# 32 adaLN half tiles moved out of the attention heads, and the sparse heads' division put on ScalarE

## The chip, the cores and the metric

One core of a Trainium2 chip runs the whole program. The metric is the device time of one execution in microseconds (us), less being better; the time before is the median of three runs. Engines are named as in the profile: PE (TensorE matmul; PEld is its weight load), DVE (VectorE), ACT (ScalarE), POOL (GpSimd), SP (SyncE, which here issues most weight loads; SPq is its queue).

## The reference

One layer of a conditioned decoder trunk, 512 positions of width 2048, all in float32. Cut to what matters here:

```
c_act = silu(c)                                   # c: one row of 2048
mod = c_act @ w_ada + b_ada                       # 6 vectors of 2048
sh1, sc1, gt1, sh2, sc2, gt2 = split(mod, 6)
h = rmsnorm(x, g_mix) * (1 + sc1) + sh1
proj = h @ w_in                                   # q, k, v, indexer, gates
y_a = stick_breaking(q_a, k_a, v_a) @ w_a         # 8 heads
y_b = sparse(q_b, k_b, v_b, indexer) @ w_b        # 8 heads, softmax over the chosen keys
x = x + (1 + gt1) * ((sigmoid(g_a) * y_a + sigmoid(g_b) * y_b) @ w_o)
h = rmsnorm(x, g_ffn) * (1 + sc2) + sh2
x = x + (1 + gt2) * conv_ffn(h, w_up, conv_w, conv_b, w_down)
out = rmsnorm(x, g_final)
```

The change touches how `mod` is summed up (its part for sh1 and sc1 is done ahead of everything, and is not touched) and the last step of the sparse heads' softmax.

## The kernel before, in words

**Weights.** Every weight tile is 128x1024 floats (512 KB). SP loads it into a buffer `raw`, ACT rounds it to `wh` (`parts`, L133), DVE takes the rest `wl = raw - wh` (L135), and PE makes three matmuls for each pair of operands (`mm3`: L143 high by high, L144 high by low of the activations, L145 low by high). Activations are split in the same way (`split`, ACT L162 and DVE L164).

**Units.** The big projections run as `unit`s (L210 on). A unit takes four tiles a11, a21, a22, a12 and makes seven products of half the width in place of eight. It forms sums of its weight tiles on DVE: s = a21+a22 (L233), s - a11 (L237), a11 - a21 (L271), a12 - s (L275), and splits each, and it adds the products up on DVE: L241, L273, L274, L277, L279. The products are called by the activation form they use, in this order: B11, T1, T2, B21, T3, B22, T4. One product of the w_o stage is 24 matmuls.

**Buffers.** `raw` has 8 buffers, handed out in a ring. Two hold c, spread over the partitions, for as long as half tiles are to be done, so six go round. A load can be issued only when the last reader of the tile that held its buffer before is done, and SP issues in order.

**Half tiles.** `ada_half` (L287) does a piece of c_act @ w_ada: SP loads a 128x1024 piece of w_ada (L289) into a `raw` buffer and one DVE instruction multiplies it by c and adds it up (L290). 96 of these are left for the time beside the stages (`ada_left`); `some_ada(n)` does the next n of them. Nothing waits for a half tile but the next user of its buffer, until `mod` is needed. In the program's order they are placed by `behind(last)`, which sets the priority of what is issued in it right behind the instruction `last`; a scheduler then orders each engine's instructions before the run, and each engine runs its own in that order, waiting where it must.

**Stages**, in order, with the half tiles of each before the change:

- x units: 32 units of w_x (the input projection). `between(0)`, right behind the sum s, takes a step of side work (rotary tables, indexer; at the end, 6 half tiles through another buffer), `between(1)`, right behind the copy of the B21 product, a step and one half tile. 38 in all.
- stick-breaking heads: two for each of 8 heads, behind `stick_2` (L858), 16 in all.
- sparse heads: `sparse_1` (logits, maxima, Exp with the sums on ACT, L884), `sparse_2` (DVE: reciprocal of the sums L888, then the four blocks of the weights times it, L890), `sparse_3` (PE transposes, L899). Two half tiles ahead of `sparse_2` and two behind its last multiplication. 32 in all. Beside the heads PE does the product with w_a.
- merge: 16 column tiles j of the product with w_b; DVE multiplies by the gate (L964) and adds (L965). One half tile behind L965 for odd j below 12, 6 in all. Behind each odd j the forms for the w_o units are made (`form_t` L175 and L176, `form_u` L181 to L183, and splits).
- w_o: 8 units; `between` also turns a finished tile (four PE transposes). One half tile in `between(1)` while there are any, 4 in all, in units 0 to 3. L996 is the residual.
- then the norm, and the feed-forward stages, which the change does not touch.

The lines that the change and the prediction speak of: `ada_half` L287 to L290, `unit` L210 to L280, `between` of the x units L632 to L636, L858, `sparse_2` L887 to L891, L938 to L944, L964 to L970, `between` of w_o L989 to L993.

Of the kernel before, what the change touches and what calls it, by code (L numbers as in the profile page):

```python
# [14 lines left out]
AF = mybir.ActivationFunctionType  # L15
ALU = mybir.AluOpType
# [60 lines left out]
def block_kernel(ctx: ExitStack, tc: tile.TileContext, A: dict, out: bass.AP):  # L77
    nc = tc.nc
# [27 lines left out]
    act = nc.scalar.activation  # L106
    tt = nc.vector.tensor_tensor
    ts = nc.vector.tensor_scalar
# [183 lines left out]
    @contextmanager  # L292
    def behind(*pins):

        with ExitStack() as stack:
            for p in pins:
                stack.enter_context(tc.issue_after(p.ins))
            yield
# [158 lines left out]
    for c in range(2):  # L457
        w = prep(A["w_qi7"][c])
        for k in range(8):
            i = 8 * c + k  # L460
# [154 lines left out]
    def some_ada(n=1, tag=("raw", 8)):  # L615
        for _ in range(n):
            if ada_left:
                ada_half(cb, *ada_left.pop(0), tag)
# [11 lines left out]
    for u in range(32):  # L630

        def between(i, *pins):  # L632
            with behind(*pins):
                next(work)
                if i:
                    some_ada()  # L636

        pair = unit(A["w_x"][u], f, between)
        for i, o in enumerate(pair):
            if u >= 16:  # L640
                sig = act(o, o, AF.Sigmoid)
            save(xd[2 * u + i], o)
# [197 lines left out]
    for hd in range(NH):  # L840
        state = stick_1(hd)
        if hd + 1 < NH:
            pairs.append([fetch(xd[2 * hd + 2]), fetch(xd[2 * hd + 3])])
        if before:
            stick_4(*before, va)
            if hd % 4 == 0:
                va = [fetch(vd[hd + b]) for b in range(NQB)]
        run(fill, 1 if hd < 4 else 2)
        if hd == NH - 1:
            cosT, sinT = (fetch(rope_d[0][:, i * S : (i + 1) * S]) for i in range(2))  # L850
            fetch_pair(0)
            for i in range(4):
                ya[i] = fetch(yad[i])
        later, last = stick_2(*state)
        run(fill)
        with behind(last):
            run(index, 3)
            some_ada(2)  # L858
        before = hd, stick_3(*state, later)
        run(fill)  # L860
    run(index, 100)
# [23 lines left out]
        return p, s, last  # L885

    def sparse_2(p, s):  # L887
        nc.vector.reciprocal(s, s)  # L888
        for b in (2, 0, 1, 3):
            last = ts(p[b], p[b], s[:, b : b + 1], None, ALU.mult)  # L890
        return last  # L891

    def sparse_3(p):
# [37 lines left out]
    for hd in range(NH):  # L931
        p, s, last = sparse_1(*pairs[hd])
        if before:
            sparse_4(*before, y)
        if hd + 1 < NH:
            pairs.append(turned(hd + 1))
        run(fill)
        with behind(last):  # L938
            some_ada(2)
        last = sparse_2(p, s)  # L940
        run(fill)
        before = hd, sparse_3(p), vb[hd // 4]
        with behind(last):
            some_ada(2)  # L944
        run(fill, 2)
    sparse_4(*before, y)
    run(fill)
# [7 lines left out]
    for j in range(KT):  # L955
        t = t2k("w", 2)
        save(t, td[j])
        g = fetch(xd[33 + 2 * j])
        merged.append(g)
        ps = acc()  # L960
        w = prep(A["w_b"][j])
        for k in range(NH):
            mm3(ps, cols(w, k), y[k], k == 0, k == NH - 1)
        tt(g, ps, g, ALU.mult)  # L964
        last = tt(g, g, t, ALU.add)  # L965
        if j % 2:
            if j < 12:
                with behind(last):
                    some_ada()
            f += forms(merged.__getitem__, j // 2, j // 2 + 1)  # L970


# [16 lines left out]
    def between(i, *pins):  # L989
        turn()  # L990
        with behind(*pins):
            if i:
                some_ada()  # L993

    def residual(c, j, x, at=slice(0, S)):
        stt(c[:, at], c[:, at], mod[:, 32 + j : 33 + j], x[:, at], ALU.mult, ALU.add)  # L996
# [577 lines left out]
```

## Time and profile before

| what | value |
|---|---|
| median of 3 runs | 2814.03 us (2813.0 to 2816.05) |
| the profiled execution's own time | 2819.28 us |
| its span, first to last instruction | 2817.4 us |
| mean granted clock of TensorE | 0.997 |
| PE, DVE, ACT, POOL busy | 98%, 86%, 52%, 11% of the span |

The busy times are averages over some fifteen stages. A stage is read in a table of windows: length, busy time of each engine, and the granted clock, of one stretch. In the timeline of an engine each row is one instruction (or a run of like ones, "x3"): its start, its duration, engine, line, operation, the tiles that it writes and reads, and in brackets how long the engine had been idle and what released it. Instructions on one engine overlap a little, so the pitch from one start to the next is somewhat less than the duration. For SP a row is the issue of a transfer; when the transfer landed is in the view of a tile. The profiled execution took 5.25 us more than the median.

### The profile page before, as it was taken

What the parts mean: (1) busy time and instruction counts of PE and PEld (TensorE: products, weight loads), DVE (VectorE), ACT (ScalarE), POOL (GpSimd) and SP (SyncE); (2) the same over time, 40 slices, a digit from 0 to 9 for tenths busy, and PEclk for the clock granted to TensorE, in tenths of its full rate; (3) what the DMA queues carried; (4) which work ended last, traced back from release to release, by engine and by line L of the source; (5) the groups of instructions that cost most, each with busy time, mean ns of one, the idle gap of its engine ahead of it and who ended that gap; (6) DMA issues with size and microseconds to landing.
All of it is one profiled execution on the core that took longest, in us unless ns stands there. A gap on an engine that the chain in (4) does not pass through costs nothing.

```text
span 2817.4 us, 47873 instructions
## 1 busy us (share of the span) xinstructions
PE 2763.3 (98%) x18780; PEld 2535.6 (90%) x18780; DVE 2427.0 (86%) x3464; ACT 1467.8 (52%) x2066; POOL 314.8 (11%) x519
## 2 busy tenths in 40 slices
PE   9999999999999999999999999999999999999997
PEld 6769999999998777889999999999999999887875
DVE  8979889888897899788878989898989897888886
ACT  5554444455556665434456555555555455546452
POOL 0100000000102011111220100000000000002022
PEclk9999999999999999999999999999999999999998
DMA  9964456655567457866763566666666436568786
GB/s 357 336 228 143 157 182 202 215 160 178 169 208 235 129 196 265 269 222 192 211 223 118 176 168 171 168 172 171 170 169 168 134 111 204 166 180 234 203 250 195
DMA packets 164045, 549.56 MB, mean 195 GB/s; under 512 B 21398, under 2 KB 21782, under 8 KB 163820
## 3 DMA queue, kind: packets, MB, share of 16 engines
q1 hardware_dynamic: 116076, 404.82, 45.0%
q0 software_dynamic: 47152, 141.30, 18.0%
q8 instruction: 147, 2.41, 0.4%
q14 instruction: 78, 0.64, 0.1%
q10 hardware_dynamic: 592, 0.39, 0.0%
HBM read 453.19 MB, written 89.83 MB: 193 GB/s over the span
## 4 chain that ended last, share of the span: by engine, by line
PE 73%; DVE 6%; DMA 4%; issue 3%; ACT 1%; POOL 0%; DVEq 0%; POOLq 0%; ACTq 0%; SPq 0%
PE att L145 12%; PE att L143 12%; PE att L144 12%; PE acc L145 10%; PE acc L143 10%; PE acc L144 10%; DVE wl L135 1%; DMA raw<-in_w_x 1%; PE acc L709 1%; PE acc L803 1%; PE outs L909 1%; DMA F<-sumd 1%; DMA F<-x1d 1%; PE acc L878 1%; DMA raw<-in_w_down 1%
## 5 line engine op out<-in xcount | busy, mean ns | idle before, releaser
L133 ACT ACTIVATE wh<-raw 128x1024 fp32r<-128x1024 f32 (+2 forms) x795 | 835.5, 1052 | 1039.2 <-PE acc L144 195.6
L135 DVE TENSOR_TENSOR wl<-raw,wh 128x1024 fp32r<-128x1024 f32 (+2 forms) x795 | 961.7, 1213 | 140.1 <-ACT wh L133 132.2
L143 PE MATMUL acc<-F,wh 128*128 128x256 f32 (+1 forms) x2504 | 727.8, 293 | 9.2 <-ACT F L162 5.0
L145 PE MATMUL acc<-F,wl 128*128 128x256 f32 (+1 forms) x2504 | 731.1, 292 | 2.1 <-DVE wl L135 2.1
L144 PE MATMUL acc<-F,wh 128*128 128x256 f32 (+1 forms) x2504 | 731.9, 292 | 0.2 <-DVE F L164 0.2
L145 PE MATMUL att<-F,wl 128*128 128x256 f32 (+1 forms) x2432 | 710.2, 292 | 2.9 <-DVE wl L135 2.9
L144 PE MATMUL att<-F,wh 128*128 128x256 f32 (+1 forms) x2432 | 710.1, 292 | 1.2 <-DVE F L164 1.2
L143 PE MATMUL att<-F,wh 128*128 128x256 f32 (+1 forms) x2432 | 706.9, 293 | 2.9 <-DVE sp L273 1.6
L143 PEld LDWEIGHTS acc<-F,wh 128*128 128x128 f32 x2504 | 479.1, 191 | 23.1 <-ACT F L162 6.8
L144 PEld LDWEIGHTS acc<-F,wh 128*128 128x128 f32 x2504 | 479.5, 191 | 11.7 <-DVE F L164 2.6
L145 PEld LDWEIGHTS acc<-F,wl 128*128 128x128 f32 x2504 | 479.3, 191 | 11.8 <-DVE wl L135 3.1
L143 PEld LDWEIGHTS att<-F,wh 128*128 128x128 f32 x2432 | 466.3, 192 | 14.8 <-ACT wh L133 3.7
L144 PEld LDWEIGHTS att<-F,wh 128*128 128x128 f32 x2432 | 466.4, 192 | 11.9 <-DVE F L164 4.3
L145 PEld LDWEIGHTS att<-F,wl 128*128 128x128 f32 x2432 | 465.9, 192 | 12.0 <-DVE wl L135 4.6
L290 DVE SCALAR_TENSOR_TENSOR raw<-raw,raw 128x1024 f32<-128x1024 f32 x154 | 186.5, 1220 | 9.1 <-ACT raw L323 7.9
L143 PE MATMUL att<-wh,F 128*128 128x512 f32 x448 | 178.0, 398 | 0.2 <-ACT wh L133 0.2
L144 PE MATMUL att<-wl,F 128*128 128x512 f32 x448 | 175.0, 391 | 0.2 <-DVE wl L135 0.2
L145 PE MATMUL att<-wh,F 128*128 128x512 f32 x448 | 174.8, 391 | 0.0
L233 DVE TENSOR_TENSOR raw<-raw,raw 128x1024 f32<-128x1024 f32 x81 | 98.9, 1221 | 28.2 <-DMA raw<-in_w_x 21.1
L144 PE MATMUL acc<-wl,F 128*128 128x512 f32 x288 | 112.9, 392 | 2.6 <-DVE wl L135 2.6
L145 PE MATMUL acc<-wh,F 128*128 128x512 f32 x288 | 112.2, 389 | 0.0
L143 PE MATMUL acc<-wh,F 128*128 128x512 f32 x288 | 111.8, 390 | 0.0
(355 smaller groups left out, 3645.1 us busy)
## 6 DMA issues: line engine op xcount, KB each, us to landing
raw<-in_w_up SPq DMA_DIRECT2D x164, 512.0 KB, 3.7
raw<-in_w_ada SPq DMA_DIRECT2D x154, 512.0 KB, 5.1
raw<-in_w_x SPq DMA_DIRECT2D x128, 512.0 KB, 4.3
raw<-in_w_down SPq DMA_DIRECT2D x104, 512.0 KB, 4.7
xd<-F POOLq DMA_DIRECT2D x64, 256.0 KB, 3.0
F<-xd POOLq DMA_DIRECT2D x64, 256.0 KB, 4.8
raw<-in_w_o SPq DMA_DIRECT2D x32, 512.0 KB, 4.4
soft<-in_w_gate SPq DMA_DIRECT2D x32, 512.0 KB, 3.8
```

Source lines behind the costliest of these rows:

```text
L133: pins["wh"] = act(wh, raw, AF.Copy)
L135: pins["wl"] = tt(wl, raw, wh.bitcast(F32), ALU.subtract)
L143: mm(ps, ah, bh, start=first, stop=False, skip_group_check=not check)
L144: mm(ps, ah, bl, start=False, stop=False, skip_group_check=not check)
L145: return mm(ps, al, bh, start=False, stop=last, skip_group_check=not check)
L233: last_v = tt(s, a21, a22, ALU.add)
L290: stt(raw, raw, 1.0, cb[half], ALU.mult, ALU.mult, accum_out=macc[:, t, half : half + 1])
L709: mm(dots[:, :W], both[:, b * P : (b + 1) * P], kiR[i][:, :W], start=i == 0, stop=i == 1)
L803: mm(o, negtri if tri else negones, i, start=False, stop=True, skip_group_check=True)
L878: mm(lg[b], q[:, b * P : (b + 1) * P], k[:, :W], start=b > 0, stop=True, skip_group_check=True)
L909: mm(o[:, b * P : (b + 1) * P], vs[kb][:, hd % 4 * HD : (hd % 4 + 1) * HD], pT[b][:, kb * P : (kb + 1) * P], start=kb == 0, stop=kb == b)
```

## The change

It moves 32 of the 96 half tiles: the stick heads' 16 and half of the sparse heads' 32 go. The x units get 16 more (in odd units also at `between(0)`), the merge 6 more (every odd j, two of them at j = 3, 7, 11, 15), the w_o units 10 more (one at `between(0)` too, so two in each of units 0 to 6). The order in which half tiles are done stays, and so does their number. In `sparse_2` the four multiplications on DVE become four ACT instructions, a Copy with the scale taken from a column of s; the reciprocal stays on DVE, and what was placed behind the last multiplication is now placed behind the reciprocal.

```diff
@@ x units, L632
         def between(i, *pins):
             with behind(*pins):
                 next(work)
-                if i:
+                if i or u % 2:
                     some_ada()
@@ stick heads, L855
         with behind(last):
             run(index, 3)
-            some_ada(2)
@@ sparse_2, L887
-        nc.vector.reciprocal(s, s)
+        last = nc.vector.reciprocal(s, s)
         for b in (2, 0, 1, 3):
-            last = ts(p[b], p[b], s[:, b : b + 1], None, ALU.mult)
+            act(p[b], p[b], AF.Copy, scale=s[:, b : b + 1])
         return last
@@ sparse heads, L938 and L943
         with behind(last):
-            some_ada(2)
+            some_ada()
         last = sparse_2(p, s)
...
         with behind(last):
-            some_ada(2)
+            some_ada()
@@ merge, L966
         if j % 2:
-            if j < 12:
-                with behind(last):
-                    some_ada()
+            with behind(last):
+                some_ada(1 + j % 4 // 3)
@@ w_o, L989
         with behind(*pins):
-            if i:
-                some_ada()
+            some_ada()
```

Two places show what it does to the order of an engine. Behind L855 the line numbers of the changed kernel are one to three less than those of before.

**DVE, from the end of one w_o unit into the next (units 1 and 2).** The first row is the split for T4, the last of the old unit; `wl_13892` (before) and `wl_13868` (after) are the split for B11 of the new unit. Before:

```order
L135 TENSOR_TENSOR wl_13839<-raw_13630,wh_13837 128x1024
L273 TENSOR_TENSOR sp_13732<-att_13624,ta_13662 128x256
L274 TENSOR_TENSOR F_13763<-sp_13732,ta_13662 128x256
L135 TENSOR_TENSOR wl_13892<-raw_13882,wh_13890 128x1024
L277 TENSOR_TENSOR F_13762<-att_13625,sp_13732 128x256
L996 SCALAR_TENSOR_TENSOR F_13762<-F_13762,mod,w_13618 128x512
L135 TENSOR_TENSOR wl_13924<-raw_13920,wh_13922 128x1024
L237 TENSOR_TENSOR raw_13920<-raw_13920,raw_13882 128x1024
```

And of the change:

```order
L135 TENSOR_TENSOR wl_13815<-raw_13603,wh_13813 128x1024
L273 TENSOR_TENSOR sp_13708<-att_13597,ta_13635 128x256
L274 TENSOR_TENSOR F_13739<-sp_13708,ta_13635 128x256
L135 TENSOR_TENSOR wl_13868<-raw_13858,wh_13866 128x1024
L290 SCALAR_TENSOR_TENSOR raw_13935,macc<-raw_13935,raw_79 128x1024
L277 TENSOR_TENSOR F_13738<-att_13598,sp_13708 128x256
L135 TENSOR_TENSOR wl_13900<-raw_13896,wh_13898 128x1024
L993 SCALAR_TENSOR_TENSOR F_13738<-F_13738,mod,w_13591 128x512
L237 TENSOR_TENSOR raw_13896<-raw_13896,raw_13858 128x1024
```

The new half tile stands two small instructions and one split behind the split for T4, and ahead of L277 and of the splits for T1 and T2 (`wl_13900` and, further on, the split of what L237 makes).

**SP, the loads of the same stretch.** Before, the four loads of unit 2 (L126) with the half tile of unit 1 ahead of them:

```order
L126 DMA raw_13630<-in_w_o 128x1024
L126 DMA raw_13632<-in_w_o 128x1024
L289 DMA raw_13773<-in_w_ada 128x1024
L126 DMA raw_13882<-in_w_o 128x1024
L126 DMA raw_13884<-in_w_o 128x1024
L126 DMA raw_13886<-in_w_o 128x1024
L126 DMA raw_13888<-in_w_o 128x1024
```

And of the change, to the first half tile of unit 2:

```order
L126 DMA raw_13603<-in_w_o 128x1024
L126 DMA raw_13605<-in_w_o 128x1024
L289 DMA raw_13676<-in_w_ada 128x1024
L289 DMA raw_13749<-in_w_ada 128x1024
L126 DMA raw_13858<-in_w_o 128x1024
L126 DMA raw_13860<-in_w_o 128x1024
L126 DMA raw_13862<-in_w_o 128x1024
L126 DMA raw_13864<-in_w_o 128x1024
L289 DMA raw_13935<-in_w_ada 128x1024
```

A unit takes seven buffers of the ring in place of six: four tiles, the sum s and two half tiles. The buffer that `raw_13935` takes is the one that `raw_13603`, a22 of the unit before, held; its last reader is that unit's split for T4, the first row of the DVE piece above.

**DVE, the end of the merge.** The first rows are the gating of j = 14 and 15 (L963, L964 of the changed kernel), then come two half tiles of j = 15, the forms of the last pair, and the first w_o unit's s, T1 and T2:

```order
L963 TENSOR_TENSOR F_13269<-acc_13271,F_13269 128x512
L164 TENSOR_TENSOR F_13208<-F_13232,F_13207 128x256
L964 TENSOR_TENSOR F_13269<-F_13269,w_13267 128x512
L290 SCALAR_TENSOR_TENSOR raw_13304,macc<-raw_13304,raw_79 128x1024
L290 SCALAR_TENSOR_TENSOR raw_13307,macc<-raw_13307,raw_86 128x1024
L175 TENSOR_TENSOR sp_13312<-F_13232 128x256
L181 TENSOR_TENSOR sp_13323<-F_13269,F_13232 128x256
L176 TENSOR_TENSOR sp_13312<-F_13269,sp_13312 128x256
L182 TENSOR_TENSOR sp_13323<-F_13269,F_13232 128x256
L233 TENSOR_TENSOR raw_13394<-raw_13358,raw_13360 128x1024
L164 TENSOR_TENSOR F_13317<-sp_13312,F_13315 128x512
L183 TENSOR_TENSOR sp_13323<-sp_13323 128x256
```

Before, L233, L237, L271 and the splits for T1 and T2 of that unit stood ahead of the last two L964; now all of them but the split for B11 stand behind the gating of j = 15 and the two half tiles.

## Rows read from the trace of the kernel before

**Rows 1.** The page's busy times over the span, with the number of instructions.

```profile
PE 2763.3 (98%) x18780; PEld 2535.6 (90%) x18780; DVE 2427.0 (86%) x3464; ACT 1467.8 (52%) x2066; POOL 314.8 (11%) x519
```

**Rows 2.** Windows of the stages that the change touches: from:to and length, busy time (and instructions) of PE, PEld, DVE, ACT and POOL, then granted clock, DMA share and GB/s. In this order: x units; stick heads; their end; sparse heads; end of the merge and first w_o unit; w_o units.

```profile
496.00:601.00 105.00, 105.00 (x878) 105.00 (x876) 93.07 (x123) 50.85 (x64) 8.62 (x16) 1.00 0.62 197
...
946.00:1051.00 105.00, 104.31 (x470) 74.92 (x469) 98.72 (x236) 62.24 (x95) 18.47 (x36) 1.00 0.59 193
1051.00:1072.00 21.00, 17.95 (x64) 11.26 (x63) 21.00 (x46) 12.90 (x26) 0.61 (x1) 0.92 0.27 85
1072.00:1189.00 117.00, 117.00 (x620) 97.11 (x619) 104.13 (x222) 56.76 (x119) 21.02 (x39) 1.00 0.86 293
...
1281.00:1302.00 21.00, 19.51 (x159) 19.21 (x160) 20.25 (x31) 10.03 (x15) 2.15 (x4) 1.00 0.48 158
1302.00:1430.00 128.00, 128.00 (x1073) 128.00 (x1073) 103.49 (x120) 63.08 (x86) 32.86 (x48) 1.00 0.72 215
```

**Rows 3.** Groups of instructions over the whole span: line, engine, operation, tiles and count, busy time and mean ns of one, then the engine's idle time just before them and what ended it.

```profile
L290 DVE SCALAR_TENSOR_TENSOR raw<-raw,raw 128x1024 f32<-128x1024 f32 x154 | 186.5, 1220 | 9.1 <-ACT raw L323 7.9 <-DMA raw<-in_w_ada 1.3
...
L387 ACT ACTIVATE ta<-F,amp 128x512 f32<-128x512 f32 x16 | 11.4, 715 | 10.9 <-DVE amp L385 10.9
L884 ACT ACTIVATE soft<-soft,m 128x384 f32<-128x384 f32 (+3 forms) x32 | 17.6, 553 | 18.3 <-DVE m L882 18.3
L890 DVE TENSOR_SCALAR soft<-soft,s 128x384 f32<-128x384 f32 (+3 forms) x32 | 10.2, 383 | 0.1
```

**Rows 4.** Timeline of PE in the w_o stage: the first matmuls of units 1, 2 and 3, each known by its change between the banks acc and att.

```profile
1300.64 0.28 PE L143 MATMUL att<-F,wh 128*128 128x256 f32 x1
1300.76 0.28 PE L144 MATMUL att<-F,wh 128*128 128x256 f32 x1
...
1321.65 0.28 PE L143 MATMUL acc<-F,wh 128*128 128x256 f32 x1
...
1342.68 0.28 PE L143 MATMUL att<-F,wh 128*128 128x256 f32 x1
```

**Rows 5.** Timeline of DVE in the same stage, from the end of unit 1 into unit 2: the sum s of unit 2 (L233), the split for T4 of unit 1, the split for B11 of unit 2, L277, the splits for T2 and B21, and the split for T4 of unit 2.

```profile
1314.72 1.23 DVE L233 TENSOR_TENSOR raw<-raw,raw 128x1024 f32<-128x1024 f32 x1 [2.11 <-DMA raw<-in_w_o]
1315.86 1.22 DVE L135 TENSOR_TENSOR wl<-raw,wh 128x1024 fp32r<-128x1024 f32 x1
...
1317.79 1.22 DVE L135 TENSOR_TENSOR wl<-raw,wh 128x1024 fp32r<-128x1024 f32 x1
1318.97 0.42 DVE L277 TENSOR_TENSOR F<-att,sp 128x256 f32<-128x256 f32 x1
...
1324.63 2.35 DVE L135 TENSOR_TENSOR wl<-raw,wh 128x1024 fp32r<-128x1024 f32 x2
...
1337.72 1.22 DVE L135 TENSOR_TENSOR wl<-raw,wh 128x1024 fp32r<-128x1024 f32 x1
```

**Rows 6.** SP's timeline in that stage (the issue of one half tile), and, of the view of the half tiles' loads between 1270 and 1440 us (three of them), the time from issue to landing.

```profile
1317.11 0.33 SPq L289 DMA_DIRECT2D raw<-in_w_ada  x1
...
DMA to landing us min/median/max: 4.7/5.0/5.2
```

**Rows 7.** The end of the merge and the first w_o unit, timeline of PE: the first matmul of w_o, and the two stops of this stretch.

```profile
1277.50 0.28 PE L143 MATMUL acc<-F,wh 128*128 128x256 f32 x1
...
1281.35 0.36 PE L143 MATMUL acc<-F,wh 128*128 128x256 f32 x1 [1.17 <-DVE F L964]
...
1292.38 0.39 PE L145 MATMUL acc<-F,wl 128*128 128x256 f32 x1 [1.14 <-DVE wl L135]
```

**Rows 8.** The same stretch, timeline of DVE: a split of activations (L164); the split for T2, ahead of the last gating (L964); one of the forms (L175).

```profile
1277.64 0.69 DVE L164 TENSOR_TENSOR F<-sp,F 128x512 fp32r<-128x512 f32 x1
...
1279.38 1.22 DVE L135 TENSOR_TENSOR wl<-raw,wh 128x1024 fp32r<-128x1024 f32 x1
1280.51 1.28 DVE L964 TENSOR_TENSOR F<-acc,F 128x512 f32<-128x512 f32 x2
...
1283.24 0.43 DVE L175 TENSOR_TENSOR sp<-F 128x256 f32<-128x256 f32 x1
```

**Rows 9.** An odd x unit, u = 21, timeline of DVE: the split for B11, the split for T1, the splits for T2 and B21.

```profile
645.92 1.22 DVE L135 TENSOR_TENSOR wl<-raw,wh 128x1024 fp32r<-128x1024 f32 x1
...
647.39 1.22 DVE L135 TENSOR_TENSOR wl<-raw,wh 128x1024 fp32r<-128x1024 f32 x1
...
651.25 2.50 DVE L135 TENSOR_TENSOR wl<-raw,wh 128x1024 fp32r<-128x1024 f32 x2
```

**Rows 10.** The same unit: PE's first matmul of it, SP's issue of the half tile that stands at its start, and the time to landing of the half tiles' loads between 560 and 860 us (21 of them).

```profile
647.57 0.28 PE L143 MATMUL att<-F,wh 128*128 128x256 f32 x1
...
644.17 0.33 SPq L289 DMA_DIRECT2D raw<-in_w_ada  x1
...
DMA to landing us min/median/max: 3.7/4.4/7.0
```

**Rows 11.** The end of the stick heads, timeline of PE: a stop, and one of the matmuls behind it.

```profile
1063.95 0.50 PE L145 MATMUL att<-F,wl 128*128 128x512 f32 x1 [1.68 <-DVE wl L135]
1064.29 0.40 PE L143 MATMUL att<-F,wh 128*128 128x512 f32 x1
...
1066.00 0.63 PE L145 MATMUL att<-F,wl 128*128 128x512 f32 x1
1066.43 0.63 PE L143 MATMUL att<-F,wh 128*128 128x512 f32 x1
```

## Prediction, made before the changed kernel ran

> **What bounds the kernel now.** I read the busy times first: PE works 98% of the span and DVE 86% [rows 1]. Only 54 us of the span are PE's to gain, so a change that moves DVE work can win little, and it loses wherever it makes PE wait. The windows by stage say where PE waits now [rows 2]: not at all in the x units (105.00 of 105), the sparse heads (117.00 of 117) and the w_o units (128.00 of 128); 0.7 us in the stick heads; but 3.05 of 21 us where the stick heads end (17.95 busy, DVE busy for all 21, clock 0.92), and 1.5 of 21 at the seam from the merge to w_o. The stages from which half tiles are taken give something at one seam alone; those to which they go have a full PE, and there the question is whether DVE still delivers in time. For that I followed PE's first matmul of each unit [rows 4, 10], DVE's splits ahead of it [rows 5, 9] and the loads [rows 6, 10].
>
> **The w_o units: +18, bounds +5 and +25.** PE's pace is 21.0 us for a unit (1300.64, 1321.65, 1342.68), at 0.12 us a matmul, so 24 of them take 2.88 [rows 4]. Added are ten half tiles of 1.22 us on DVE [rows 3]. Their work alone would fit: DVE is busy 103.49 of 128 us [rows 2]. Their place does not. The one at the start of a unit takes the buffer that a22 of the unit before frees, so its load can be issued only when that unit's split for T4 ends: 1315.86 + 1.22 = 1317.08, and SP issues the next load, today a half tile too, at 1317.11 [rows 5, 6]. It lands 5.0 us later (4.7 to 5.2) [rows 6]. But in DVE's order the half tile stands right behind the split for B11, which starts at 1317.79, and ahead of L277 at 1318.97 [rows 5]. DVE would wait until 1317.11 + 5.0 = 1322.1, work to 1323.25, and start L277 4.3 us later than now. All behind it moves along: the splits for T1 and T2, then L271 and L275, whose ends free the buffers for the next loads. Spare: the split for T2 ends at 1324.63 + 1.14 = 1325.77 [rows 5]; PE uses it at 1321.65 + 2 x 2.88 for B11 and T1, + 0.44 for four transposes, + 0.24 for the two matmuls that need only the other half = 1328.1. That is 2.3 us, so the first unit with a half tile at its start loses 4.3 - 2.3 = 2.0 at most; since part of the spare can be rebuilt in front of the unit I count 0.45. From then on DVE and its loads set the pace. Between the splits for T4 of two units lie 1337.72 - 1315.86 = 21.86 us today [rows 5], already more than PE's 21.0; DVE's waits in between are waits for loads (L233 waits 2.11 for its tile) whose issue hangs on DVE's own splits, so they do not shrink when DVE is late. With 4.3 more, less 0.4 to 1.6 us of waits for ACT and PE that do shrink, a unit takes 24.6 to 25.7; I take 24.5, 3.5 over PE's pace. Five more units: 0.45 + 5 x 3.5 = 18. Below: the load takes the 3.7 us of the x units' quickest [rows 10] and a unit loses about 1. Above: nothing of the 4.3 is absorbed, 5 to 6 units.
>
> **The seam from the merge to w_o: +6, bounds +1 and +8.** PE ends the merge at 1277.5 and has two stops today, 1.17 (for a bank that L964 must read first) and 1.14 [rows 7]. The new order has the gating of j = 15 earlier, then two half tiles, four forms, L233, three activation splits, and then the split for T1. From 1277.5: gating and a small split 1.5; half tiles 2 x 1.22; forms 4 x 0.33; L233 1.14; L164, L183, L164 1.5; the split 1.14: 1286.6 (pitches of such rows [rows 8]). Today T1 starts at 1281.35. T2's split is behind one more activation split, a third half tile, L237, L271 and itself: 5.2 more, 1291.8, where T1 leaves PE at about 1289.5. The two stops become about 6.3 and 2.0 in place of 2.3 together: +6. Below: DVE makes up part of it, and only the three half tiles count, 3.7 - 2.3 = 1.4. Above: the third half tile's load, too, is late by 2 us.
>
> **The x units: +5, bounds 0 and +10.** Sixteen half tiles, 20 us of DVE work, in a stage where DVE has 93.07 of 105 us filled [rows 2]: it fits, but again by place. In unit 21 the load can go at 644.17, lands 4.4 us later at 648.6 (3.7 to 7.0) [rows 10], and with 1.22 of work the split for T1 starts at 649.8 in place of 647.39 [rows 9]: 2.4 later. The split for T2 ends now at 651.25 + 1.22 = 652.47 and is used at 647.57 + 2 x 2.88 + 0.24 = 653.57 [rows 9, 10]: 1.1 spare, so PE stops 1.3 us. In units 11, 13 and 15 the indexer's side work lies over the load, and I count nothing. The other thirteen lie between 0 and this unit's 1.3 to 1.6; I take 0.4 for each. A load at the upper end, 7.0 us, would double it.
>
> **The end of the stick heads: -4.5, bounds -1.7 and -5.4.** Four half tiles stood around this seam, 4.9 us of a DVE that is busy for all 21 us [rows 2]; two stay. The stop of 1.68 for a split [rows 11] should go, and so most of the other waits, 3.05 in all; the matmuls behind it come at 0.43 us in place of 0.24, about eight of them, 1.6 us; with the 0.7 of the stage before it that is 5.4 at most. The stop alone is 1.7. I take 4.5, because nearly all of it follows from DVE being full.
>
> **The sparse heads and ScalarE: 0, bounds 0 and +7.5.** PE is full there, so DVE's 16 fewer half tiles and its 10.2 us of multiplications [rows 3] win nothing. ACT's four copies have no row of before; the nearest are its Exp over the same four shapes, 0.553 us each, and a copy with a scale from memory over 128x512, 0.715 [rows 3]. Four take 2.2 us for 1.27 on DVE, before the transposes. ACT is busy 56.76 of 117 us and PE has w_a's product beside it, so I count nothing; uncovered, 0.94 x 8 = 7.5. The Trainium skill, page "ScalarE: Activation LUTs", section "Rules for kernel authors", speaks against this half of the change: it puts multiplications on VectorE, as the faster engine for them. The rows of Exp and of DVE's multiplication agree (0.553 and 0.383); by that rule alone the stage would lose, which is the last rival below.
>
> **Sum.** 18 + 6 + 5 - 4.5 = +24.5. The profiled execution took 2819.28 us, 5.25 more than the median of the runs; on its own time that is 2843.8, on the median of 2814.03, 2838.5, and I predict 2838.
>
> **Rivals.**
> - *The waits are mostly hidden.* DVE idles 24 of 128 us in w_o; if the late loads come mostly out of that, w_o costs 5, the seam 3, x 1.5, and the stick heads give 4.5: +5, 2819. Against it: DVE's idle time there is itself waiting for loads.
> - *Faster: the seams give back and nothing is late.* It decides at a shift of 2.3 us in w_o and 1.1 in x: if the loads land soon enough for that (about 3.0 and 3.1 us after their issue), no split is late. Then the end of the stick heads gives 5.4, and the gating of j = 15, now earlier, ends the stops of 2.3 at the merge: -7.7, 2806. Against it: no load of these views landed before 3.7 us.
> - *The clock falls.* In the 21 us at the end of the stick heads PE was 85% busy and had 0.92 [rows 2]; w_o units of 24.5 us for 21.0 of work are 86% busy. At 0.92 the stage's 128 us cost 10 more, the seam 1.7: 2850. Against it: the x units' neighbours at 1.00 have short stops too. The Trainium skill, page "TensorE: Matmul & The Clock Gate", Part 1, says that the slow clock is the default and that activity lifts it; the rows at 0.92 agree.
> - *ScalarE holds the transposes*: +7.5 on the forecast, 2846.
>
> **Chances.** The forecast's case 0.68; hidden 0.15; faster 0.06; clock 0.07; ScalarE 0.04. The range runs from the lowest sum (5 + 1 + 0 - 5.4, about 2814.5) to near the highest sum and the clock's case: 2813 to 2852. A difference of 0.2%, 5.6 us, is about what a measurement of this kernel can tell from none: faster is below 2808.4, slower above 2819.7. Faster: the third case and a little of the first, 0.07. Same: two thirds of the hidden case and the low end of the first, 0.13. Slower: 0.80.
>
> **What would show it.** In the changed kernel's trace: L290 waiting on DVE for its own load at the start of units; PE stops for the split for T2 in w_o, and bank changes some 24.5 us apart; the 1063.95 stop gone, with clock 1.00 there; 32 more ACT rows and no stop of PE's transposes for them. Wrong if the w_o units keep 21.0 us, or if L290's load there was issued earlier than the end of the split for T4.

## The result and the profile after

The changed kernel took 2838.71 us (median of 5 runs, 2835.64 to 2840.75) against 2814.55 of before (5 runs): a ratio of 1.0085, interval 1.0074 to 1.0096, slower by 24.2 us. 2838 was forecast. Its profiled execution has a span of 2837.2 us; PE is busy for 2767.3 of it. Against the profile of before, a slow one, the span is 19.8 us longer: PE is busy for 4.0 us more and stands still for 15.8 us more, so four fifths of the loss is PE standing still.

PE executes the same 18,780 matmuls in nearly the same order in all these kernels, so the loss can be placed by the times at which the 700th, 6,250th, 7,300th, 8,230th and 9,250th start. Worked out from PE's rows of each trace, in us between these marks:

| kernel | x units | stick heads and their end | sparse heads, merge, seam | w_o units 1 to 6 |
|---|---|---|---|---|
| before | 697.5 | 234.2 | 183.8 | 121.8 |
| the change | 697.9 | 227.2 | 195.5 | 137.0 |
| x and stick heads alone | 699.5 | 228.9 | 184.5 | 121.8 |
| w_o alone | 692.6 | 233.3 | 186.5 | 138.0 |
| division alone | 695.5 | 233.4 | 183.3 | 121.8 |
| merge alone | 694.6 | 234.7 | 195.6 | 121.8 |
| both at the middle of w_o | 695.5 | 232.5 | 184.6 | 123.4 |
| early load in w_o | 694.5 | 231.5 | 184.2 | 122.7 |
| merge without j = 15 | 693.4 | 232.9 | 189.4 | 121.8 |
| smaller move | 693.5 | 229.7 | 188.6 | 121.8 |
| smaller move, early load | 695.4 | 227.9 | 184.8 | 124.0 |
| the change, put right | 701.2 | 227.3 | 184.3 | 122.3 |

The x units vary by some us from run to run even where nothing in them is changed: 692.6 to 697.5, mean 694.7 over the nine such rows. The profile of before had the slowest of them, 2.8 us over the mean; this is about half of the 5.25 us that it stood above the median. Against the means of the untouched rows (694.7; stick heads 233.2 over seven; merge and seam 183.9 over three, before, x alone and division alone; w_o 121.8), the change has +3.2, -6.0, +11.6 and +15.2: +24.0, and the medians differ by 24.2. The +3.2 is no larger than the spread of the untouched x units; that they lose something is told by all three kernels with the added half tiles there, 697.9, 699.5 and 701.2, lying above all nine.

**The w_o units.** The order of DVE around the start of unit 4 answers to [rows 5]: split for T4, for B11, the new half tile, L277, then the splits for T2 and B21, the split for B22, and the next unit's L233. DVE's timeline of the changed kernel:

```profile
1369.81 1.22 DVE L135 TENSOR_TENSOR wl<-raw,wh 128x1024 fp32r<-128x1024 f32 x1
...
1371.74 1.22 DVE L135 TENSOR_TENSOR wl<-raw,wh 128x1024 fp32r<-128x1024 f32 x1
1374.65 1.23 DVE L290 SCALAR_TENSOR_TENSOR raw<-raw,raw 128x1024 f32<-128x1024 f32 x1 [1.70 <-DMA raw<-in_w_ada]
...
1375.80 0.42 DVE L277 TENSOR_TENSOR F<-att,sp 128x256 f32<-128x256 f32 x1
...
1381.20 2.35 DVE L135 TENSOR_TENSOR wl<-raw,wh 128x1024 fp32r<-128x1024 f32 x2
...
1387.34 1.22 DVE L135 TENSOR_TENSOR wl<-raw,wh 128x1024 fp32r<-128x1024 f32 x1
1393.41 1.23 DVE L233 TENSOR_TENSOR raw<-raw,raw 128x1024 f32<-128x1024 f32 x1 [4.85 <-DMA raw<-in_w_o]
```

The split for T4 ends at 1371.03, SP issues the half tile's load at 1371.06, and DVE stands 1.70 us for it, ahead of L277. Then it stands 4.85 us for the next unit's weights, where [rows 5] had 2.11. PE's timeline of the same unit, its start (the answer to [rows 4]), its two stops and the start of the next:

```profile
1374.46 0.28 PE L143 MATMUL acc<-F,wh 128*128 128x256 f32 x1
...
1382.47 0.38 PE L145 MATMUL acc<-F,wl 128*128 128x256 f32 x1 [1.42 <-DVE wl L135]
...
1396.25 0.36 PE L143 MATMUL acc<-F,wh 128*128 128x256 f32 x1 [1.82 <-DVE sp L273]
...
1399.19 0.28 PE L143 MATMUL att<-F,wh 128*128 128x256 f32 x1
```

One stop is for the split for T2, as forecast, the other stands ahead of the product T4, whose bank L273 must read first: 24.73 us for this unit, 21.0 before. Over the whole stage 5.5 us of PE's stops are of the first kind and 6.0 of the second, which the prediction did not name. SP's timeline in that unit (issues, and the time from the first to the last of a run):

```profile
1371.06 5.18 SPq L289 DMA_DIRECT2D raw<-in_w_ada  x2
1380.65 7.13 SPq L126 DMA_DIRECT2D raw<-in_w_o  x4
```

The view of the half tiles' loads between 1270 and 1440 us (14 of them): who waited for them, in us and times, and how long they took to land:

```profile
  DVE raw L290: 8.5, 6
...
DMA to landing us min/median/max: 3.5/3.6/3.9
```

The same of the weights' loads between 1302 and 1440 us:

```profile
  DVE raw L233: 23.8, 6
...
DMA to landing us min/median/max: 5.4/6.7/9.4
```

And of the weights' loads in the kernel before, between 1302 and 1430 us:

```profile
  DVE raw L233: 6.7, 3
...
DMA to landing us min/median/max: 3.6/4.7/6.6
```

The half tiles landed sooner than in [rows 6] (3.6 for 5.0), the weights later (6.7 for 4.7). The four of a unit go out within 7.13 us here, in unit 2 of before within 8.77; whether that is why they land later is taken up with the run that has both half tiles at the middle.

**The seam** from the merge to w_o, PE's timeline, the answer to [rows 7]:

```profile
1275.74 0.38 PE L143 MATMUL acc<-F,wh 128*128 128x256 f32 x1 [1.04 <-ACT F L162]
1276.40 0.38 PE L144 MATMUL acc<-F,wh 128*128 128x256 f32 x1 [0.27 <-DVE F L164]
...
1282.86 0.58 PE L143 MATMUL acc<-F,wh 128*128 128x256 f32 x1 [5.96 <-ACT wh L133]
...
1284.44 0.58 PE L145 MATMUL acc<-F,wl 128*128 128x256 f32 x1 [0.79 <-DVE wl L135]
1284.82 0.41 PE L143 MATMUL acc<-F,wh 128*128 128x256 f32 x1
1285.03 0.41 PE L144 MATMUL acc<-F,wh 128*128 128x256 f32 x1
...
1290.91 0.39 PE L143 MATMUL acc<-F,wh 128*128 128x256 f32 x1 [0.99 <-ACT wh L133]
```

Stops of 9.05 us stand in place of 2.3. The long one is ahead of T1, for the rounded form of the sum s. DVE makes s (L233) behind the two half tiles of j = 15 and four forms:

```profile
1276.86 1.22 DVE L290 SCALAR_TENSOR_TENSOR raw<-raw,raw 128x1024 f32<-128x1024 f32 x1
...
1278.01 1.22 DVE L290 SCALAR_TENSOR_TENSOR raw<-raw,raw 128x1024 f32<-128x1024 f32 x1
...
1280.49 1.22 DVE L233 TENSOR_TENSOR raw<-raw,raw 128x1024 f32<-128x1024 f32 x1
```

And ACT rounds it behind that:

```profile
1281.74 1.06 ACT L133 ACTIVATE wh<-raw 128x1024 fp32r<-128x1024 f32 x1 [0.32 <-DVE raw L233]
```

Behind the stops of 5.96 and 0.79 the matmuls come 0.21 us apart in place of 0.12, from 1284.82 to 1289.5: 22 of them, 2.0 us. The granted clock of that stretch, in a window with the columns of [rows 2], is 0.50, the lower of the clock's two levels (1.2 GHz):

```profile
1284.80:1289.50 4.70, 4.70 (x23) 4.70 (x23) 4.67 (x6) 1.06 (x1) 0.00 (x0) 0.50 0.38 112
```

**The windows** of stages shown in [rows 2], columns as there (the stick heads, their end, the seam, and w_o with its new end at 1441):

```profile
946.00:1051.00 105.00, 104.88 (x471) 75.03 (x470) 86.05 (x212) 64.00 (x97) 18.50 (x36) 1.00 0.35 117
1051.00:1072.00 21.00, 20.55 (x102) 16.29 (x103) 20.39 (x46) 17.00 (x38) 3.21 (x6) 1.00 0.40 142
...
1281.00:1302.00 21.00, 17.37 (x118) 16.78 (x119) 18.68 (x23) 8.80 (x11) 0.00 (x0) 0.78 0.50 166
1302.00:1441.00 139.00, 127.43 (x1039) 125.77 (x1039) 105.87 (x130) 60.67 (x84) 31.96 (x47) 0.99 0.69 219
```

At the end of the stick heads PE is busy 20.55 of 21 us (17.95 before) at a clock of 1.00 (0.92). The seam's clock fell to 0.78. The division's new rows, ACT's copies and the transposes that wait for them (groups over the whole span):

```profile
L889 ACT ACTIVATE soft<-soft,s 128x384 f32<-128x384 f32 (+3 forms) x32 | 15.3, 551 | 2.0 <-DVE s L887 1.9
...
L898 PE MATMUL acc<-const,soft 128*128 128x128 f32 x80 | 11.1, 275 | 0.4 <-ACT soft L889 0.4
```

A copy takes 0.551 us, as the Exp over the same shapes in [rows 3] had led one to expect, and PE waited 0.4 us for them in all.

### The profile page after: what moved, and what is told of

The parts are those of the page before. It is cut to its first block, busy times and chain, and to the rows that moved or that the text cites. A ratio compares the mean times of both kernels' runs of the same rounds, so it can differ in the third digit from the quotient of the medians.

```text
span 2837.2 us, 47875 instructions
## 1 busy us (share of the span) xinstructions
PE 2767.3 (98%) x18780; PEld 2539.0 (89%) x18780; DVE 2417.2 (85%) x3432; ACT 1480.8 (52%) x2098; POOL 314.3 (11%) x519
## 4 chain that ended last, share of the span: by engine, by line
PE 75%; DVE 9%; DMA 7%; issue 7%; ACT 1%; POOL 1%; DVEq 0%; POOLq 0%; ACTq 0%; SPq 0%
PE att L145 12%; PE att L143 12%; PE att L144 12%; PE acc L144 11%; PE acc L145 11%; PE acc L143 10%; DVE wl L135 3%; DVE raw L290 2%; DMA raw<-in_w_va 1%; DMA raw<-in_w_down 1%; DMA raw<-in_w_ada 1%; DVE F L164 1%; ACT wh L133 1%; PE acc L709 1%; DMA raw<-in_w_x 1%
## 5 line engine op out<-in xcount | busy, mean ns | idle before, releaser
L144 PEld LDWEIGHTS acc<-F,wh 128*128 128x128 f32 x2504 | 481.2, 192 | 11.6 <-DVE F L164 2.5
L290 DVE SCALAR_TENSOR_TENSOR raw<-raw,raw 128x1024 f32<-128x1024 f32 x154 | 186.9, 1217 | 25.8 <-DMA raw<-in_w_ada 17.3
L233 DVE TENSOR_TENSOR raw<-raw,raw 128x1024 f32<-128x1024 f32 x81 | 98.6, 1217 | 43.6 <-DMA raw<-in_w_o 24.0
```

The costliest lines, as they stand in the source:

```text
L144: mm(ps, ah, bl, start=False, stop=False, skip_group_check=not check)
L233: last_v = tt(s, a21, a22, ALU.add)
L290: stt(raw, raw, 1.0, cb[half], ALU.mult, ALU.mult, accum_out=macc[:, t, half : half + 1])
```

## The experiments

Four kernels did one part of the change each; for the w_o and the merge part, as many half tiles as were added were left out of the middle sparse heads, where PE is full. In the kernels whose edit adds a line ahead of the merge, the line numbers there are one more than those of before (L965 is the gating L964). The halving of the sparse heads' half tiles was not run by itself.

**x units and stick heads alone.**

```diff
-                if i:
+                if i or u % 2:
                     some_ada()
...
-            some_ada(2)          # stick heads
```

> The stick heads' 16 half tiles go to the x units (as in the change); sparse heads, merge, w_o and the division stay as before. My forecast's terms: x units +5 and end of the stick heads -4.5, so 2815 (same). Rival, read from the changed kernel's trace (x units -0.1 against before, stick heads and their end -6.6): 2808, faster by 0.2%. If the end of the stick heads gains only because sparse heads lose half tiles or multiplications too, the stop of 1.7 us for a split there stays and the time is 2814 to 2819.

Measured 2815.2 us (11 runs) against 2812.95, ratio 1.0008 (1.0000 to 1.0017): where the forecast's two terms put it; the 2808 read from a single trace is out. By the table x has +4.8 and the stick heads -4.3. The reading that gave x -0.1 had compared with a profile of before whose x units happened to be slow. The -4.3 is itself a sum: at the 7,050th matmul, where the stick heads end, this kernel has gained 6.9 us on the profile of before, as much as the change (7.0); by the 7,400th, in the sparse heads, 3.0 us of it are given back, 1.9 of that as PE's transposes wait for DVE's multiplications. The change, with fewer half tiles in the sparse heads and the copies on ACT, keeps it.

**w_o alone.**

```diff
         with behind(*pins):
-            if i:
-                some_ada()
+            some_ada()
...
-            some_ada(2)
+            if not 2 <= hd < 7:
+                some_ada(2)      # sparse heads, second place
```

> Only the w_o units change: 14 half tiles in units 0 to 6, as in the change; ten fewer in the sparse heads 2 to 6; all else as before. Theory (place of the half tile at the unit's start, its load waiting for the last split of the unit before): +15 to +18 in units 1 to 7, and 1 to 3 more at the seam, where a third half tile stands ahead of T2's split: 2830 to 2835. Rival (the w_o units are late only because the merge and its seam hand them over late): under +5, 2815 to 2819.

Measured 2833.2 us against 2812.95, ratio 1.0065 (1.0052 to 1.0077). The w_o units take 138.0 us as in the whole change, so they need no late seam to be late; the seam itself has 2.6 more. DVE's groups between 1300 and 1430 us show the two waits:

```profile
L290 DVE SCALAR_TENSOR_TENSOR raw<-raw,raw 128x1024 f32<-128x1024 f32 x10 | 12.2, 1221 | 9.1 <-DMA raw<-in_w_ada 9.1
L233 DVE TENSOR_TENSOR raw<-raw,raw 128x1024 f32<-128x1024 f32 x5 | 6.1, 1226 | 21.4 <-DMA raw<-in_w_o 21.4
```

**Division alone.**

```diff
-        nc.vector.reciprocal(s, s)
+        last = nc.vector.reciprocal(s, s)
         for b in (2, 0, 1, 3):
-            last = ts(p[b], p[b], s[:, b : b + 1], None, ALU.mult)
+            act(p[b], p[b], AF.Copy, scale=s[:, b : b + 1])
```

> Only the division goes to ScalarE, the half tiles stay where they were. Theory (PE has other work beside it, DVE is relieved of 1.3 us per head): 0, 2812 to 2816, the stop at the end of the stick heads a little shorter at most. Rival (the four copies hold the transposes, 0.94 us for each of 8 heads): +7.5, 2822.

Measured 2815.7 us (11 runs) against 2812.95, ratio 1.0007 (0.9998 to 1.0016): no change that can be told. The sparse heads' column is 183.3 for 183.8. The rival's 7.5 us are excluded.

**Merge alone.**

```diff
-                if j < 12:
-                    some_ada()
+                some_ada(1 + j % 4 // 3)
...
+            if not 2 <= hd < 5:
                 some_ada(2)      # sparse heads, second place
```

> Only the merge changes: 12 half tiles, two of them behind j = 15, as in the change; six fewer in the sparse heads 2 to 4. My forecast's term for the seam without the third half tile of w_o unit 0: +3 to +5, 2817 to 2820. From the changed kernel's trace, where the seam lost 11 with a fall of the clock behind the long stop: +8 to +10, 2823 to 2825, if the two half tiles of j = 15 and the order they bring are what makes the stop. If it is the w_o unit's own half tile: under +2.

Measured 2827.06 us against 2812.95, ratio 1.0045 (1.0033 to 1.0058): +14, more than either text said; the table has 11.7 of it at the merge and its seam. PE's two longest stops there:

```profile
1273.17 0.47 PE L143 MATMUL acc<-F,wh 128*128 128x512 f32 x1 [2.83 <-DVE F L965]
...
1290.15 0.58 PE L143 MATMUL acc<-F,wh 128*128 128x256 f32 x1 [5.96 <-ACT wh L133]
```

The second is the one of the change, to the hundredth. The first is new: L965 (the gating of a column tile) is late because in DVE's order a split of w_o's first tile stands ahead of it, and that waits. DVE's row of it, in the timeline of this kernel:

```profile
1269.99 1.23 DVE L135 TENSOR_TENSOR wl<-raw,wh 128x1024 fp32r<-128x1024 f32 x1 [3.55 <-ACT wh L133]
```

ACT's row of the same tile:

```profile
1268.90 1.06 ACT L133 ACTIVATE wh<-raw 128x1024 fp32r<-128x1024 f32 x1 [4.20 <-DMA raw<-in_w_o]
```

And SP's issues ahead of that:

```profile
1254.08 4.14 SPq L289 DMA_DIRECT2D raw<-in_w_ada  x2
1261.91 14.91 SPq L126 DMA_DIRECT2D raw<-in_w_o  x4
```

w_o's first load goes out at 1261.91, behind two half tiles of the same queue and ring. The half tiles keep nobody waiting themselves; the weight tile behind them is late, and DVE, in order, is late with it. But two half tiles stand there in the changed kernel too, as SP's timeline of it shows:

```profile
1249.45 4.14 SPq L289 DMA_DIRECT2D raw<-in_w_ada  x2
1257.27 12.86 SPq L126 DMA_DIRECT2D raw<-in_w_o  x4
```

There the same split waits 1.49 us and PE 0.77, so the two loads in front are not enough to make this stop.

**The same half tiles in w_o, both at the middle of a unit.** Base: w_o alone.

```diff
-            some_ada()
+            if i:
+                some_ada(2)
```

> As the w_o run, the same 14 half tiles in w_o units 0 to 6, but both of a unit behind the copy of the B21 product, none at its start. Theory (it is the place: the half tile at the start waits for a load that can go only when the unit before is done): units back to 21.0 to 21.6 us, 2813 to 2818. Rival (it is the amount: 1.2 us more of DVE work and a sixth 512 KB load per unit): as the w_o run, 2830 to 2835.

Measured 2816.8 us (11 runs) against 2814.54, ratio 1.0011 (1.0002 to 1.0020). The amount is the same, the w_o units take 123.4 us in place of 138.0. The place is the cause. SP's issues of one unit's weights in this kernel:

```profile
1347.34 4.90 SPq L126 DMA_DIRECT2D raw<-in_w_o  x4
```

The view of the weights' loads between 1300 and 1430 us:

```profile
  DVE raw L233: 13.1, 6
...
DMA to landing us min/median/max: 5.1/6.1/7.0
```

The four loads stand closer together than in the change (4.90 us for 7.13) and still land sooner (6.1 for 6.7), so their spacing alone does not set how late they land. And DVE stands 13.1 us for them, twice as long as before, with PE's units at 21.0 to 21.5 us from unit 2 on: without a half tile at the unit's start, such waits cost next to nothing.

**An earlier load for the half tile at the start.** Base: w_o alone; `ada_half` only loads and hands back its multiplication.

```diff
         a22 = load(src[3], w)
+        early()                  # takes the half tile's buffer, loads it
         a12 = load(src[1], w)
...
             if i:
                 some_ada()
+            elif held:
+                held.pop()()     # the multiplication, where it was
```

> As the w_o run, the half tile is still used at the unit's start, but its tile is taken and loaded ahead of the unit's fourth weight tile (a12), so it gets a buffer that the unit before frees earlier, and a12 the later one. Theory (the wait is for the buffer that the split for T4 frees): L290 does not wait for its load, units 21.0 to 21.8 us, 2813 to 2819. Rival (the position on DVE ahead of the splits for T1 and T2 is enough): 2825 or more, with PE stops for those splits and no DVE wait for the load.

Measured 2817.14 us (11 runs) against 2814.54, ratio 1.0007 (0.9998 to 1.0016); w_o units 122.7 us. The multiplication still stands in `between(0)`, at the start of the unit. DVE's groups between 1300 and 1430 us, to be read against those of w_o alone (L234 and L291 are L233 and L290 there):

```profile
L234 DVE TENSOR_TENSOR raw<-raw,raw 128x1024 f32<-128x1024 f32 x6 | 7.4, 1225 | 2.8 <-DMA raw<-in_w_o 2.8
L291 DVE SCALAR_TENSOR_TENSOR raw<-raw,raw 128x1024 f32<-128x1024 f32 x11 | 13.4, 1220 | 1.1 <-DMA raw<-in_w_ada 1.1
```

Both waits are gone, 30.5 us to 3.9, with the same work. So what costs is the buffer that the load has to wait for, not the work. One reservation keeps the buffer from being shown by itself: the scheduler also put the multiplication a few instructions further ahead, right behind L234 in the units 2 and 3, so position and load moved together by that much.

**Merge without the half tiles of j = 15.** Base: merge alone.

```diff
+                if j < 15:
                     some_ada(1 + j % 4 // 3)
```

> As the merge run, but without the two half tiles behind j = 15 (they stay in a sparse head); those behind j = 13 and the doubled ones of 3, 7 and 11 stay. Theory (two half tiles and the order they bring make the seam's long stop of 6.1 us and the slow clock behind it): the stop of 3.0 at the second last column tile stays, the long one goes, 2817 to 2820. Rival (the stop comes from the gating of j = 15 being ordered ahead of the first unit's weight sums, whatever stands behind it): 2824 or more.

Measured 2820.08 us (11 runs) against 2814.54, ratio 1.0021 (1.0013 to 1.0030). The stop of 5.96 is gone, the first one stays:

```profile
1271.11 0.73 PE L143 MATMUL acc<-F,wh 128*128 128x512 f32 x1 [3.28 <-DVE F L965]
...
1282.37 0.38 PE L143 MATMUL acc<-F,wh 128*128 128x256 f32 x1 [1.45 <-DVE F L965]
```

The column of merge and seam falls from 195.6 to 189.4. What is left, 5.5 over the untouched 183.9, is mostly the first stop and slow matmuls behind it. Without the two half tiles DVE's order also has L237 and L271 ahead of the last gating again, as before, so the run does not part their 2.4 us of work from the order that they bring.

**A smaller move.** Six half tiles from the last three stick heads, to places that I took to be free.

```diff
+            if hd < 5:
                 some_ada(2)      # stick heads
...
             if j < 12:
                 with behind(last):
-                    some_ada()
+                    some_ada(1 + j % 4 // 3)
```

> A smaller move: six half tiles, those of the last three stick heads, go to the merge (a second one at j = 3, 7 and 11) and to the w_o units 4 to 6 at their middle; x units, sparse heads and the division as before. Theory (the end of the stick heads gains 5 to 6 once the half tiles ahead of it are gone, and places with a free ring and DVE cost nothing): 2806 to 2809, faster. Rival (the gain needs all 16 gone, or is given back in the sparse heads, as 2 us were when all 16 went to the x units): 2811 to 2815.

Measured 2816.86 us (11 runs) against 2814.54, ratio 1.0009 (1.0000 to 1.0018). My theory fell. The stick heads gave 3.5 (229.7), but the merge took 4.7 (188.6):

```profile
1267.84 0.77 PE L143 MATMUL acc<-F,wh 128*128 128x512 f32 x1 [2.92 <-DVE F L965]
```

It is a stop in the same place, with the doubled half tiles of j = 3, 7 and 11 as the only addition to the merge; which of the three is enough was not tried. The wait inside it is another one. Here, and in the run without j = 15, no half tile stands in SP's queue between the merge's last loads and w_o's first. DVE's row ahead of L965:

```profile
1265.87 1.23 DVE L135 TENSOR_TENSOR wl<-raw,wh 128x1024 fp32r<-128x1024 f32 x1 [1.40 <-ACT wh L133]
```

ACT's row of that tile:

```profile
1264.78 1.06 ACT L133 ACTIVATE wh<-raw 128x1024 fp32r<-128x1024 f32 x1 [3.12 <-PE acc L144]
```

DVE waits 1.40 us, and ACT waited for PE, not for a load. What the three kernels have in common is that work of w_o's first unit (splits, and in two of them the sum L233) stands ahead of the gating on DVE; what makes it late differs, and no run parts the causes. The stick heads' part needs a word too: 6.3 us are gained where they end, and 1.7 of them are given back in the sparse heads, as in the x run.

**The smaller move with the early load.** The merge as before; w_o has 14 with the early load, taken from stick heads 5 to 7 (6) and sparse heads 0 and 1 (4).

```diff
+            if hd < 5:
                 some_ada(2)      # stick heads
...
-            some_ada(2)
+            some_ada(1 if hd < 2 else 2)   # sparse heads, both places
```

> As the run with the early load in w_o (14 half tiles there, the first of a unit loaded ahead of a12), and the ten that it takes come from the last three stick heads (6) and the first two sparse heads (4); merge and x units as before. Theory (the end of the stick heads gives 5.2, w_o costs 1 to 2): 2809 to 2812, faster than before by 0.1 to 0.2%. Rival (the sparse heads or the seam give it back, as in the smaller move): 2814 to 2817.

Measured 2811.33 us (11 runs, 2808.96 to 2815.11) against 2814.42, ratio 0.9989 (0.9980 to 0.9998): faster than the kernel before by 0.1%, with an interval that only just leaves out no change. The stick heads give 5.3 (227.9), w_o costs 2.2.

**The change with its two costly parts put right**: the early load in w_o, and the merge as before (its six extra half tiles in sparse heads 5 to 7).

> The change, with its two costly parts put right: the w_o units' first half tile is loaded ahead of a12, and the merge has the six half tiles of before (the six others stay in sparse heads 5 to 7). x units, stick heads, division as in the change. Theory (the w_o units' waits of 15 and the seam's 11 are all of the loss; x +3, end of the stick heads -6 stay): 2811 to 2816, the same as before. Rival (the parts act on one another, so that some of the loss stays): 2820 or more.

Measured 2816.72 us (11 runs) against 2814.42, ratio 1.0009 (1.0001 to 1.0018). Of 24 us, 2 are left: x +6.5 (701.2), stick heads -5.9, the rest within 1. So the two parts together are the loss. They do not simply add up, though: the four kernels with one part each lose 2.3, 20.3, 2.8 and 14.1 us by their medians, each good to some 3 us: 39 in all, where the whole change loses 24. Some of that shows in the table: the merge run's stop of 2.83 us is one of 0.77 in the change, the w_o run has 2.6 us at a seam where the merge run has 11.7 and the change 11.6, and the x run gives back a gain that the change keeps. The rest is not placed.

## Why the prediction held, step by step

- **What bounds the kernel** held in the main: PE was full in the sparse heads, taking half tiles from the middle ones gave nothing, and the gain came where the stick heads end. But that gain keeps only if the sparse heads behind it are relieved too: with all their half tiles there, 3.0 us of it went again in the x run and 1.7 in the smaller move. The smaller move with the early load, which takes four half tiles from the first two sparse heads too, kept it.
- **w_o, +18 forecast, +15.2 measured.** The mechanism was right, and the two runs that move the half tile or its load show it: the half tile at the start waits for a buffer that the split for T4 frees. Sizes were off against each other. Its load landed after 3.6 us, not 5.0, so DVE stood 1.6 to 1.7 us for it in the units 2 to 6 and L277 was some 2.9 late, not 4.3. And I had the waits at L233 stay as they were; they grew from 6.7 to 23.8 us, since the weights' loads went out later in a unit (6.2 us behind the start of unit 4, 2.4 behind that of unit 2 of before) and landed later too. That lateness made the stops ahead of T4, 6.0 us, more than those for T2, 5.5, which were the only ones that I had forecast. Units 2 to 6 took 22.1 to 26.1 us, not an even 24.5.
- **The seam, +6 forecast, +11.6 measured**: the term that was mis-sized most. The order that I had read did make it. The stops came to 9.05 us where I had 8.3, spread otherwise: 6.75 at T1 for 6.3, 0.99 at T2 for 2.0 (my own times there give 2.3), and 1.31 ahead of both, for splits of the last column tiles, where I had none. What I left out is what follows a stop: 2.0 us of matmuls at half the clock, which I had kept in the clock rival alone, some 1.5 us in all of longer pitches at the restarts, and a stop of 0.8 in the merge. In the three runs with doubled half tiles in the merge that last stop was about 3 us; why it was short in the whole change stays open.
- **x units, +5 forecast, +3.2 in the profile of the change**, and +4.8 and +6.5 in the two other runs that have it.
- **End of the stick heads, -4.5 forecast, -6.0 measured**, past my bound of -5.4. Against the profile of before the change gains 7.0 us by the 7,050th matmul, 1.0 of it in the stage before and 6.0 between the 7,000th and that one, and nothing further on. The bound counted the stops and the slow matmuls and left out the longer pitches behind each stop, some 2 us by the same rows.
- **Division, 0 forecast**: 0.4 us of waits. The Trainium skill, page "ScalarE: Activation LUTs", section "Rules for kernel authors", puts multiplications on VectorE as the faster engine; the rows agree on the speed (0.551 for 0.383 us, in float32), and the run of the division alone shows no loss from it that can be told here: in the changed kernel PE waited 0.4 us for the copies, having other work.
- **The rivals.** That the waits would be mostly hidden is out: the w_o run alone has +20. The faster case is out, though its mechanism (a shift below the spare) fits what the early load brings about. The clock rival was right for 2.0 us at the seam and for a few matmuls in w_o, not for the stage: it ran at 0.99. (Its price of 10 us takes 8% of 128; 128 us of work at 0.92 would lose 11.)

The terms were off by -2.8, +5.6, -1.8 and -1.5; that the sum came out at the measured time within 1 us is their cancelling, and luck: a term that was off by 5.6 is hidden in it.

## What to carry to other kernels

Work that fits by its busy time (12 us of DVE in a stage with 24 us idle) can cost more than its own length by its place (15 us): ask of every added load which buffer it takes, whose last reader frees that, and what stands behind the waiting instruction on its in-order engine. Taking the buffer one load sooner, ahead of a tile that is used later, gave back 15.3 of the 16.2 us that the w_o run lost in these units. And when parts of a few us are compared, one profile of before is not enough: an untouched stage moved by up to 5 us between profiles, and that alone made a loss of 3 to 6 us look like none (697.9 against 697.5). Nor do parts that were measured one by one have to add up to the whole: 39 us here, for a loss of 24.

## What the runs showed of the hardware

- After PE stops of 5.96 and 0.79 us matmuls of 128x256 came 0.21 us apart in place of 0.12, from 1284.82 to 1289.5, at a granted clock of 0.50, the lower of the clock's two levels (1.2 GHz). Stops of 1 to 2 us in w_o mostly left the clock at its upper level, 0.99 for the stage. But a stop of 2.17 us at the seam of the w_o run was followed by 16 matmuls at the slow pitch, at a granted clock of 0.52 (the window below). The Trainium skill, page "TensorE: Matmul & The Clock Gate", Part 1, has the slow clock as the default that activity lifts; the trace agrees.
- Loads of the same 512 KB landed after 3.6 us (median) for the half tiles of the change, the second of a pair going out when the first had landed, and after 6.7 for its weights, four within 7.13 us; but after 6.1 where four went out within 4.90. How close the loads stand is not all that sets it.

```profile
1278.00:1281.40 3.40, 3.40 (x16) 3.40 (x17) 3.40 (x8) 0.42 (x1) 1.08 (x2) 0.52 0.47 134
```
